# A hybrid decoder layer on one core: sums of weight quarters issued singly, token sums inside a product, a last product by token tiles

## The chip, the core and the metric

The kernel runs on one core of a Trainium2 chip. The core's engines work side by side, each through its own list of instructions in order: TensorE (PE) for matrix products, with its weight loads (PEld) overlapped; VectorE (DVE) for element work; ScalarE (ACT) for copies, casts and functions; GpSimd (POOL), here for the rsqrt powers, some fills and some DMAs; SyncE (SP), whose list issues nearly all DMAs. A DMA that must wait for something holds everything behind it in the list that issues it. The metric is the device time of one execution in microseconds (us). TensorE's clock is granted by a throttle; the trace gives it as a share of full speed.

## The reference, cut to what matters

One layer (DEPTH is 1) over 1024 tokens and 16 meta tokens, width 1024, all in float32:

```python
h = layer_norm(concat(meta, x), emb_ln_g, emb_ln_b)
p = h @ w_in[l]                       # one input projection for four mixers
y_pool, y_rw, y_lru, y_ml = ...       # pooling, RWKV-7, RG-LRU, mLSTM
mix = jnp.concatenate([y_pool, y_rw, y_lru, y_ml], axis=-1) @ w_out[l]
h = layer_norm(ALPHA * h + mix, ln1_g[l], ln1_b[l])
ff = jnp.square(jax.nn.relu(h @ mlp_w1[l])) @ mlp_w2[l]
h = layer_norm(ALPHA * h + ff, ln2_g[l], ln2_b[l])
return h[:, N_META:]
```

The MLP is 1024 to 4096 and back to 1024.

## The kernel before

**Products.** Every float32 operand is split into a high part (cast on ACT) and a low part (original minus high, on DVE); a product is three matmuls, high x high, high x low and low x high (`mm3`, the matmuls of L1149). `split` (L125, L126) does this for data, `load_w` (L117, L120, L121) loads one 512 KB tile of weights by SP and splits it. Two raw tiles are held, so SP is at most two weight loads ahead of the split.

**The mixers.** The eight token tiles of 128 are taken in four blocks of two. A list written by hand (`PLAN`, then `STEPS`) sets the order in which the program's steps are written: `e` embedding and its LayerNorm, `S` parts of the input projection, `P`, `I`, `C` the RWKV mixer (the inverse of a triangular system, with small round trips through memory: `dr`, `XTm`, `SA`, `XT`), `L` the RG-LRU, `O` the pooling, `M` the mLSTM, `W` six parts of the output projection with the first LayerNorm (its rsqrt power runs on POOL, L133) and the store of `h1d`, `T` and `G` the first-layer product of the first half of the tokens, and `Z`. A scheduler then makes each engine's final list from the written order and the waits.

**The Z steps.** The MLP saves products in the manner of Strassen: the tokens are two halves, the weight matrices two by two quarters, and seven products of sums replace eight. Four of them need sums of quarters of the second weight w2, kept in memory as `rd1` to `rd4`, each in four pieces of 1 MB (in listings, `rd_0_207` to `rd_3_210` are rd1's pieces, 211 to 214 rd2's, 215 to 218 rd3's, 219 to 222 rd4's; `in_w` is then w2). `Z0` to `Z3` make one piece of each (`w2_sums`): SP copies a quarter to rd1, POOL issues a DMA that adds another quarter to it (an accumulating DMA, L1181); the same for rd3; then SP copies rd1 to rd2 (L1180) and POOL accumulates, then rd2 to rd4 and POOL accumulates. Each copy of one sum to the next waits for the accumulation before.

**Behind the mixers.** `mlp_sums` makes five operands of token sums (`t0` to `t4`, in the code `tops`) in transposed layout: it loads the second token half's tiles of `h1d`, transposes them on PE (L1207), copies them on ACT (L1209), forms differences with the first half's transposed tiles `h1t` on DVE (six per tile, L1213 to L1218) and splits five results per tile. Then comes `down_product("11")`, the first second-layer product, with operands loaded (L1298, L1304) and split for two of 16 steps at a time into a ring of 8 high and 8 low tiles; then 16 `mlp_set` (the first-layer products of the sums) and six more `down_product`: 21, s2, n1, s3, s4 and 22. In a `down_product` each group of two steps runs six matmuls on each of four banks of PSUM, bank after bank; a bank belongs to a token tile. While 22 runs, the first four token tiles are normed (`acc[0..3]`, L1344); after it, for each of the other four, the bank is added (L1349) and the second LayerNorm follows (statistics L145, L146; L160 and L161 apply it) and the store (L162).

Of the kernel before, what the change touches and what calls it, by code (L numbers as in the profile page):

```python
# [9 lines left out]
F32 = mybir.dt.float32  # L10
F32R = mybir.dt.float32r
# [25 lines left out]

PLAN = ("e0 Srw0.0 Srw0.1 k Srw0.2 Srw0.3 Srw0.4 Srw0.5 Srw0.6 Slp0.0 P0 I0 C0.0 Slp0.1 C0.1 Slp0.2 C0.2 "
# [52 lines left out]
class Trunk:  # L91
# [36 lines left out]
    def rsqrt(self, out, var, eps, pool, w):  # L128

        nc = self.nc  # L130
        rows = out.shape[0]
        nc.vector.tensor_scalar(out, var, eps, None, op0=ALU.add)  # L132
        nc.gpsimd.tensor_tensor(out, out, self.mhalf[0:rows, 0:w], op=ALU.pow)  # L133

    def layer_norm(self, t, rows, g, b, junk=None, pool=False, out=None, cut=1):

        nc = self.nc
        rs = self.smp.tile([P, 1], F32, name="ln_rs")
# [1 line left out]
        x = t[0:rows]  # L140
        mean, var = mv[0:rows, 0:1], mv[0:rows, 1:2]
        if junk is None:
            st = self.smp.tile([P, 2, 6], F32, name="ln_st")
            for i in range(2):
                nc.vector.bn_stats(st[0:rows, i], x[:, i * 512:(i + 1) * 512])  # L145
            nc.vector.bn_aggr(mv[0:rows], st[0:rows].rearrange("p a b -> p (a b)"))  # L146
            self.rsqrt(rs[0:rows], var, LN_EPS, self.smp, 1)
        else:
            sm = self.smp.tile([P, 2], F32, name="ln_sm")
            nc.scalar.activation(junk[0:rows], x, AF.Identity, accum_out=sm[0:rows, 0:1])  # L150
            nc.scalar.activation(sm[0:rows, 1:2], sm[0:rows, 0:1], AF.Copy, scale=-1.0 / D ** 1.5)
            nc.scalar.activation(mean, sm[0:rows, 0:1], AF.Copy, scale=1.0 / D)
            nc.scalar.activation(junk[0:rows], x, AF.Square, scale=D ** -0.5, bias=sm[0:rows, 1:2], accum_out=var)
            nc.gpsimd.tensor_tensor(rs[0:rows], var, self.eps[0:rows], op=ALU.add)
            nc.gpsimd.tensor_tensor(rs[0:rows], rs[0:rows], self.mhalf[0:rows, 0:1], op=ALU.pow)
# [126 lines left out]
    def program(self, top):  # L282
# [36 lines left out]
        self.rws, self.mls, self.lrs = ([{} for b in range(nb)] for i in range(3))  # L319
        M, M2 = ExitStack(), ExitStack()  # L320
        for st in STEPS:
            t, i = (st.split(".") + ["0"])[0:2]
            k, b, i = t[0], int(t[-1]) if t[-1].isdigit() else None, int(i)
            if k == "k":
# [5 lines left out]
            elif k == "T":  # L330
                self.mlp_in()
            elif k == "G":
                self.mlp_first(int(t[1:]))
            elif k == "Z":
                self.w2_sums(b)
            elif k == "C":
                self.rwkv_chunk(b, i)
            elif k == "M":
                if i == 0:
                    self.mlstm_pre(b)  # L340
                else:
                    self.mlstm_chunk(b, i - 1)
            elif k == "S":
                self.sweep(b, t[1:3], i)
            elif k == "W":
                self.w_out(b, i)
            else:
                {"e": self.emb, "P": self.rwkv_pre, "I": self.rwkv_inverse, "L": self.lru, "O": self.pool}[k](b)
        X.close()
        M2.close()  # L350
        L.close()
        psc = psum(top, "psC")
        self.bank = [psc.tile([P, 512], F32, name="bank%d" % i) for i in range(8)]
        U, U2, DD = ExitStack(), ExitStack(), ExitStack()
        self.wcp = pool(DD, "wc")
        self.ring = 8
        self.p1s = [pool(DD, "p1s%d" % i).tile([P, 512], F32, name="p1s") for i in range(4)]
        self.tp = pool(U, "tops")
        tmp = ExitStack()
        self.tmp = pool(tmp, "tprep", "right")  # L360
        self.mlp_sums()
        self.down_product("11", 0, self.bank[4:8], True)
        for i in range(4):
            nc.scalar.copy(self.p1s[i], self.bank[4 + i])
        tmp.close()
# [802 lines left out]
        nc.vector.tensor_tensor(m, m, m, op=ALU.mult)  # L1168
        nc.sync.dma_start(self.md["11"][k], m)

    def w2_sums(self, j):

        nc, w2 = self.nc, self.a["w2"]
        q = lambda f, d: w2[16 * f + 4 * j:16 * f + 4 * j + 4, :, 512 * d:512 * d + 512].rearrange("n p c -> (n p) c")
        r = {i: self.rd[i][j] for i in self.rd}
        jobs = ((1, q(0, 0), q(0, 1)), (3, q(0, 1), q(1, 1)), (2, r[1], q(1, 1)), (4, r[2], q(1, 0)))
        last = self.last_dma
        for i, first, more in jobs:
            with self.tc.issue_after(last):
                nc.sync.dma_start(r[i], first)  # L1180
            nc.gpsimd.dma_start(r[i], more, accum_op=ALU.add)  # L1181

    def half_split(self, pool, name, out_h, out_l, src, neg=False):
        nc = self.nc
        if neg:
            nc.scalar.activation(out_h, src, AF.Copy, scale=-1.0)
            nc.vector.scalar_tensor_tensor(out_l, src, -1.0, out_h.bitcast(F32), op0=ALU.mult, op1=ALU.subtract)
        else:
            self.split(out_h, out_l, src)

    def mlp_sums(self):

        nc, tmp = self.nc, self.tmp
        self.tops = [[self.tp.tile([P, 4, 512], F32R, name="t%d%s" % (q, x)) for x in "hl"] for q in range(5)]
        bh, bl = self.h1t
        v = lambda x: x.rearrange("p (a b) -> p a b", b=P)
        tt = nc.vector.tensor_tensor
        for i in range(4):
            cs = slice(i * P, (i + 1) * P)
            x = tmp.tile([P, D], F32, name="h1x", bufs=2)  # L1200
            nc.sync.dma_start(x, self.h1d[4 + i])
            b = []
            for half in range(2):
                pt = self.bank[2 * (i % 2) + half]
                for j in range(4):
                    kt = half * 4 + j
                    nc.tensor.transpose(pt[:, j * P:(j + 1) * P], x[:, kt * P:(kt + 1) * P], self.ident)  # L1207
                y = tmp.tile([P, 512], F32, name="b%d2" % half)
                nc.scalar.copy(y, pt)  # L1209
                b.append(y)  # L1210
            t1, t2, t3, t4 = (tmp.tile([P, 512], F32, name="tt%d" % q) for q in range(4))
            h = lambda z, k: z[:, 4 * k:4 * k + 4, cs].bitcast(F32)
            tt(v(t1), v(b[0]), h(bh, 0), op=ALU.subtract)  # L1213
            tt(v(t1), v(t1), h(bl, 0), op=ALU.subtract)
            tt(t2, b[1], t1, op=ALU.subtract)  # L1215
            tt(t3, b[0], b[1], op=ALU.subtract)
            tt(v(t4), h(bh, 1), v(t2), op=ALU.subtract)
            tt(v(t4), v(t4), h(bl, 1), op=ALU.add)  # L1218
            for q, z in ((1, t2), (0, t1), (2, t3), (4, b[1]), (3, t4)):
                self.half_split(tmp, "t", self.tops[q][0][:, :, cs], self.tops[q][1][:, :, cs], v(z), neg=(q == 4))  # L1220

        for i in range(2):
            nc.tensor.matmul(self.bank[i], lhsT=self.identr, rhs=self.tops[0][0][:, 0], start=True, stop=True)

    def pair(self, src):
        hi = self.wcp.tile([P, 512], F32R, name="wh", bufs=self.ring)
# [61 lines left out]
        for q, y in zip(("n1", "s2", "s3", "s4"), o):  # L1288
            nc.sync.dma_start(self.md[q][k], y)

    def down_product(self, q, w, banks, start, group=2):

        nc, w2 = self.nc, self.a["w2"]
        for g in range(0, NS, group):
            ops = []
            for k in range(g, g + group):
# [14 lines left out]
    def mlp_out(self, ap):  # L1311
# [26 lines left out]
        for i in R4:  # L1338
            tt(v7[i], X[i], self.p1s[i], op=ALU.add)
            tt(v7[i], v7[i], y5[i], op=ALU.add)  # L1340
            stt(acc[4 + i][:, hi], acc[4 + i][:, hi], ALPHA, v7[i], op0=ALU.mult, op1=ALU.subtract)
        self.down_product("22", 4, X, False)
        for i in R4:
            tt(v[i], v[i], Y[i], op=ALU.add)  # L1344
            stt(acc[i][:, hi], acc[i][:, hi], ALPHA, v[i], op0=ALU.mult, op1=ALU.subtract)
# [1 line left out]
        for i in R4:  # L1347
            t = 4 + i
            tt(acc[t][:, lo], acc[t][:, lo], X[i], op=ALU.add)  # L1349
# [54 lines left out]
```

## Time and profile before

| | us |
|---|---|
| median of three runs | 1393.0 (1391.18 to 1403.27) |
| the profiled execution | 1390.15 |
| its span in the trace | 1388.1 |
| PE busy | 1249.0 (90%) |
| DVE busy | 868.5 (63%) |
| ACT busy | 616.7 (44%) |
| POOL busy | 91.7 (7%) |

The profiled execution is 2.85 us below the median of the runs. Its mean granted clock is 0.931 of full speed. Times in the trace count from the span's start. The mixers end near 814, the products run from 848 to 1372, and the final LayerNorms end at 1388. A row of the trace names the source line, the engine, the operation and the tiles as output<-input; in brackets is the engine's idle time before it, and what ended it.

### The profile page before, as it was taken

Reading aid. Unit: us, or ns where it says so; the run is one execution under the profiler, and the core shown is the slowest. Engines: PE = TensorE matmul, PEld = TensorE weight load, DVE = VectorE, ACT = ScalarE, POOL = GpSimd, SP = SyncE. Lnnn points to the kernel's source line nnn. Section 1 sums busy time; section 2 is a strip of 40 time slices with the busy share of each in tenths; the row PEclk is TensorE's granted clock in tenths of the full one; section 3 lists DMA queues with packets and bytes.
Section 4 is the critical chain, followed back from the end, with each engine's and each line's share of the span. In section 5 each row is a group of like instructions: output and inputs, shape, how many; then the busy total and the mean of one; then the engine's idle time right before and its main releaser. Section 6 shows DMA issues by size and latency. Waiting matters only on the chain. (4 is left out here: it accounts for less than half of the span.)

```text
span 1388.1 us, 21003 instructions
## 1 busy us (share of the span) xinstructions
PE 1249.0 (90%) x7619; PEld 1065.3 (77%) x7619; DVE 868.5 (63%) x2122; ACT 616.7 (44%) x1128; POOL 91.7 (7%) x117
## 2 busy tenths in 40 slices
PE   4999988999986977999699666999999999999995
PEld 3989877898986965775587654888888888888884
DVE  8847645776634654554576477676767556545697
ACT  5436464452355442434233244465666643443431
POOL 3110010000100010002001000000000000000011
PEclk9999997899997977997889787999999999999998
DMA  7422267252496469527943455667666587656662
GB/s 249 164 81 74 73 170 195 96 144 62 137 253 188 137 201 224 183 69 202 240 137 108 131 191 174 187 222 243 226 229 235 197 304 250 195 187 200 192 220 114
DMA packets 122599, 245.84 MB, mean 177 GB/s; under 512 B 28768, under 2 KB 35568, under 8 KB 122368
## 3 DMA queue, kind: packets, MB, share of 16 engines
q1 hardware_dynamic: 114048, 227.73, 49.5%
q0 software_dynamic: 8448, 16.78, 7.3%
q8 instruction: 60, 0.98, 0.3%
q14 instruction: 43, 0.35, 0.1%
HBM read 193.07 MB, written 84.94 MB: 200 GB/s over the span
## 5 line engine op out<-in xcount | busy, mean ns | idle before, releaser
L126 DVE TENSOR_TENSOR wl<-raw,wh 128x512 fp32r<-128x512 f32 x240 | 151.5, 685 | 121.3 <-ACT wh L125 121.2
L125 ACT CAST wh<-raw 128x512 fp32r<-128x512 f32 x240 | 133.5, 618 | 196.0 <-PE bank L1149 189.7
L452 PE MATMUL b<-hTh,wlo 128*128 128x256 f32 (+1 forms) x672 | 195.5, 291 | 1.9 <-DVE wlo L121 1.9
L451 PE MATMUL b<-hTl,whi 128*128 128x256 f32 (+1 forms) x672 | 196.5, 293 | 0.6 <-DVE hTl L126 0.4
L450 PE MATMUL b<-hTh,whi 128*128 128x256 f32 (+1 forms) x672 | 195.9, 292 | 0.2 <-ACT hTh L125 0.2
L1149 PE MATMUL bank<-wl,wh 128*128 128x512 f32 x448 | 175.4, 392 | 4.2 <-DVE wl L126 4.2
L1149 PE MATMUL bank<-wh 128*128 128x512 f32 x448 | 175.3, 393 | 1.1 <-ACT wh L125 1.1
L1149 PE MATMUL bank<-wh,wl 128*128 128x512 f32 x448 | 175.2, 391 | 0.0
L121 DVE TENSOR_TENSOR wlo<-wraw,whi 128x1024 fp32r<-128x1024 f32 x90 | 109.7, 1220 | 102.6 <-ACT whi L120 101.1
L120 ACT CAST whi<-wraw 128x1024 fp32r<-128x1024 f32 x90 | 94.3, 1047 | 146.4 <-PE b L451 42.6
L452 PEld LDWEIGHTS b<-hTh,wlo 128*128 128x128 f32 x672 | 129.8, 193 | 3.8 <-DVE wlo L121 2.7
L451 PEld LDWEIGHTS b<-hTl,whi 128*128 128x128 f32 x672 | 129.8, 193 | 3.8 <-issue 1.5
L450 PEld LDWEIGHTS b<-hTh,whi 128*128 128x128 f32 x672 | 130.0, 193 | 1.5 <-ACT hTh L125 0.7
L1149 PEld LDWEIGHTS bank<-wl,wh 128*128 128x128 f32 x448 | 84.7, 189 | 22.7 <-DVE wl L126 5.2
L1149 PEld LDWEIGHTS bank<-wh 128*128 128x128 f32 x448 | 84.8, 190 | 19.2 <-ACT wh L125 1.5
L1149 PEld LDWEIGHTS bank<-wh,wl 128*128 128x128 f32 x448 | 84.7, 189 | 17.4
L1127 PE MATMUL b<-whi,mixh 128*128 128x256 f32 x256 | 76.3, 300 | 12.3 <-ACT mixh L125 9.6
L1128 PE MATMUL b<-wlo,mixh 128*128 128x256 f32 x256 | 77.6, 303 | 2.2 <-DVE wlo L121 2.2
L133 POOL TENSOR_TENSOR ln_rs<-ln_rs,mhalf 128x1 f32<-128x1 f32 (+1 forms) x22 | 31.0, 1410 | 709.4 <-DVE ln_rs L132 709.4
L1129 PE MATMUL b<-whi,mixl 128*128 128x256 f32 x256 | 76.6, 301 | 0.0
L126 DVE TENSOR_TENSOR wl<-s,wh 128x512 fp32r<-128x512 f32 x64 | 43.7, 688 | 33.0 <-ACT wh L125 33.0
L1127 PEld LDWEIGHTS b<-whi,mixh 128*128 128x128 f32 x256 | 51.6, 202 | 13.3 <-ACT mixh L125 9.9
(424 smaller groups left out, 2562.9 us busy)
## 6 DMA issues: line engine op xcount, KB each, us to landing
wraw<-in_w_in SPq DMA_DIRECT2D x42, 512.0 KB, 3.5
rd<-in_w POOLq DMA_DIRECT2D x16, 1024.0 KB, 10.9
wraw<-in_w_out SPq DMA_DIRECT2D x32, 512.0 KB, 3.6
raw<-in_w SPq DMA_DIRECT2D x32, 512.0 KB, 4.3
raw<-rd SPq DMA_DIRECT2D x64, 256.0 KB, 3.8
md<-m SPq DMA_DIRECT2D x48, 256.0 KB, 2.0
raw<-md SPq DMA_DIRECT2D x48, 256.0 KB, 4.0
raw<-in_w SPq DMA_DIRECT2D x48, 256.0 KB, 4.1
```

The costliest lines, as they stand in the source:

```text
L120: nc.scalar.copy(hi, raw)
L121: (nc.gpsimd if pool else nc.vector).tensor_tensor(lo, raw, hi.bitcast(F32), op=ALU.subtract)
L125: self.nc.scalar.copy(hi, src)
L126: self.nc.vector.tensor_tensor(lo, src, hi.bitcast(F32), op=ALU.subtract)
L133: nc.gpsimd.tensor_tensor(out, out, self.mhalf[0:rows, 0:w], op=ALU.pow)
L450: nc.tensor.matmul(pt, lhsT=wh[:, ks], rhs=hh[:, kt, 0:nb], start=(kt == 0), stop=False)
L451: nc.tensor.matmul(pt, lhsT=wh[:, ks], rhs=hl[:, kt, 0:nb], start=False, stop=False)
L452: nc.tensor.matmul(pt, lhsT=wl[:, ks], rhs=hh[:, kt, 0:nb], start=False, stop=(kt == 7))
L1127: nc.tensor.matmul(pt, lhsT=xh, rhs=wh, start=(kt == 0), stop=False)
L1128: nc.tensor.matmul(pt, lhsT=xh, rhs=wl, start=False, stop=False)
L1129: nc.tensor.matmul(pt, lhsT=xl, rhs=wh, start=False, stop=(kt == 7))
L1149: mm = lambda *p, **k: self.nc.tensor.matmul(*p, skip_group_check=True, **k)
```

## The change

Three things change. Behind the change the line numbers of the profile shift by some 5 to 14.

1. The four Z steps go. Their 32 transfers become single steps (`SUMS`; C a copy by SP, A an accumulation by POOL), put into `STEPS` one at every fourth place from place 16: all copies of rd1 and rd3, all their accumulations, the copies of rd2, its accumulations, then rd4. A copy is placed in SP's list right behind the weight load written last, an accumulation in POOL's behind the rsqrt power written last.
2. `mlp_sums(i)` works on one token tile: it loads that tile of both halves, forms four differences in token layout before the transposes (on POOL for tiles 0 and 1, on DVE for 2 and 3), transposes five results (20 transposes per tile, 80 in all, where there were 32), and splits them straight from PSUM. Between the four calls stand two groups each of product 11.
3. The ring is 20 from `mlp_out` on, and the last product's last group holds eight of the 16 steps, so that each bank gets its last 24 matmuls in one run. The statistics of the half of each last tile that is ready earlier are taken ahead.

```diff
+SUMS = [(k, i, j) for q in ((1, 3), (2,), (4,)) for k in "CA" for i in q for j in range(4)]
+for n, z in enumerate(SUMS):
+    STEPS.insert(16 + 4 * n, z)
...
-        nc.gpsimd.tensor_tensor(out, out, self.mhalf[0:rows, 0:w], op=ALU.pow)
+        self.last_pool = nc.gpsimd.tensor_tensor(out, out, self.mhalf[0:rows, 0:w], op=ALU.pow).ins
...
+            if isinstance(st, tuple):
+                self.w2_sum(*st)
+                continue
...
-        self.mlp_sums()
-        self.down_product("11", 0, self.bank[4:8], True)
+        for i in range(4):
+            self.mlp_sums(i)
+            self.down_product("11", 0, self.bank[4:8], True, range(4 * i, 4 * i + 4, 2))
...
+        self.wcp, self.ring = pool(DD, "wd"), 20
...
-        for i, first, more in jobs:
-            with self.tc.issue_after(last):
-                nc.sync.dma_start(r[i], first)
-            nc.gpsimd.dma_start(r[i], more, accum_op=ALU.add)
+    def w2_sum(self, k, i, j):
+        if k == "C":
+            with self.tc.issue_after(self.last_dma):
+                nc.sync.dma_start(r[i][j], {1: q(0, 0), 3: q(0, 1), 2: r[1][j], 4: r[2][j]}[i])
+        else:
+            with self.tc.issue_after(self.last_pool):
+                nc.gpsimd.dma_start(r[i][j], {1: q(0, 1), 3: q(1, 1), 2: q(1, 1), 4: q(1, 0)}[i], accum_op=ALU.add)
...
+        nc.sync.dma_start(x2, self.h1d[4 + i])
+        nc.sync.dma_start(x1, self.h1d[i])
+        tt = (nc.gpsimd if i < 2 else nc.vector).tensor_tensor
+        tt(t1, x2[:, lo], x1[:, lo], op=ALU.subtract)
+        tt(t2, x2[:, hi], t1, op=ALU.subtract)
+        tt(t3, x2[:, lo], x2[:, hi], op=ALU.subtract)
+        tt(t4, x1[:, hi], t2, op=ALU.subtract)
+        for q, z in ((4, x2[:, hi]), (0, t1), (1, t2), (2, t3), (3, t4)):
+            pt = self.bank[self.nt % 4]
+            for j in range(4):
+                nc.tensor.transpose(pt[:, j * P:(j + 1) * P], z[:, j * P:(j + 1) * P], self.ident)
...
+            nc.vector.bn_stats(sts[i][:, 1], acc[4 + i][:, hi])
-        self.down_product("22", 4, X, False)
+        self.down_product("22", 4, X, False, [0, 2, 4, 6, 8])
```

What this does to the engines' lists shows at three places. On SP, around the step Z1 of before (`wraw` are weight loads, `x<-h0d` a load of the residual):

```order
L1180 DMA rd_1_208<-in_w 512x512
L1180 DMA rd_1_216<-in_w 512x512
L117 DMA wraw<-in_w_in 128x1024
L1180 DMA rd_1_212<-rd_1_208 16x16384
L117 DMA wraw<-in_w_out 128x1024
L1180 DMA rd_1_220<-rd_1_212 16x16384
L117 DMA wraw<-in_w_out 128x1024 x2
```

and the corresponding place in the changed list, about the output projection of block 1:

```order
L122 DMA wraw<-in_w_in 128x1024
L1191 DMA rd_0_211<-rd_0_207 16x16384
L1124 DMA x<-h0d_66 128x1024
L122 DMA wraw<-in_w_in 128x1024
L1191 DMA rd_1_212<-rd_1_208 16x16384
L122 DMA wraw<-in_w_out 128x1024 x3
L1078 DMA yd_316<-sc_4695 128x2x256
L122 DMA wraw<-in_w_out 128x1024
L122 DMA wraw<-in_w_in 128x1024
L1191 DMA rd_2_213<-rd_2_209 16x16384
```

Between a copy and the next one there are now one or more other loads, and rd2's copies stand there alone: rd1's accumulations were issued far ahead. In the same way the copies of rd1 and rd3 stand earlier among input weight loads, the first copy of rd3 and some of rd1 just ahead of the small transfers of the first RWKV inverse.

On POOL, the end of the list before, with the rsqrt powers of the last LayerNorms (`ln_rs`; in one row with those of the final norms) and of the last head norms:

```order
L133 TENSOR_TENSOR ln_rs<-ln_rs,mhalf 128x1
L133 TENSOR_TENSOR ml_rs<-ml_rs,mhalf 128x4
L133 TENSOR_TENSOR ln_rs<-ln_rs,mhalf 128x1
L133 TENSOR_TENSOR rw_rs<-rw_rs,mhalf 128x4 x2
L133 TENSOR_TENSOR ln_rs<-ln_rs,mhalf 128x1 x10
```

and now (`tt` are the token differences, `h1x` the loaded token tiles):

```order
L1194 DMA rd_2_221<-in_w 512x512
L138 TENSOR_TENSOR rw_rs<-rw_rs,mhalf 128x4
L1210 TENSOR_TENSOR tt_8590<-h1x_8585 128x512
L1208 TENSOR_TENSOR tt_8588<-h1x_8585,h1x_8584 128x512
L1209 TENSOR_TENSOR tt_8589<-h1x_8585,tt_8588 128x512
L1211 TENSOR_TENSOR tt_8591<-h1x_8584,tt_8589 128x512
L1210 TENSOR_TENSOR tt_8724<-h1x_8719 128x512
L1208 TENSOR_TENSOR tt_8722<-h1x_8719,h1x_8718 128x512
L1209 TENSOR_TENSOR tt_8723<-h1x_8719,tt_8722 128x512
L1211 TENSOR_TENSOR tt_8725<-h1x_8718,tt_8723 128x512
L138 TENSOR_TENSOR ln_rs<-ln_rs,mhalf 128x1 x10
```

The two accumulations of rd4 and the eight differences now stand ahead of the last ten powers, two of which belong to the first LayerNorm of the last block.

On DVE, the norms of the last token tiles at the end of the list before (`L1349` adds the bank):

```order
L1349 TENSOR_TENSOR acc_11534<-acc_11534,bank_8549 128x512
L145 BN_STATS ln_st<-acc_11534 128x6
L1349 TENSOR_TENSOR acc_11535<-acc_11535,bank_8550 128x512
L146 BN_AGGR ln_mv<-ln_st 128x2
L145 BN_STATS ln_st<-acc_11535 128x6
L132 TENSOR_SCALAR ln_rs<-ln_mv 128x1
L160 SCALAR_TENSOR_TENSOR acc_11534<-acc_11534,ln_mv,bc_ln2g 128x1024
L145 BN_STATS ln_st<-acc_11535 128x6
L161 SCALAR_TENSOR_TENSOR acc_11534<-acc_11534,ln_rs,bc_ln2b 128x1024
L146 BN_AGGR ln_mv<-ln_st 128x2
L1349 TENSOR_TENSOR acc_11536<-acc_11536,bank_8551 128x512
```

and now, where `L1356` adds the bank and `st_` are the statistics:

```order
L1356 TENSOR_TENSOR acc_11561<-acc_11561,bank_8550 128x512
L153 BN_STATS st_11577<-acc_11561 128x6
L154 BN_AGGR ln_mv<-st_11577 128x2
L137 TENSOR_SCALAR ln_rs<-ln_mv 128x1
L168 SCALAR_TENSOR_TENSOR acc_11561<-acc_11561,ln_mv,bc_ln2g 128x1024
L169 SCALAR_TENSOR_TENSOR acc_11561<-acc_11561,ln_rs,bc_ln2b 128x1024
L1356 TENSOR_TENSOR acc_11562<-acc_11562,bank_8551 128x512
L153 BN_STATS st_11578<-acc_11562 128x6
L154 BN_AGGR ln_mv<-st_11578 128x2
L137 TENSOR_SCALAR ln_rs<-ln_mv 128x1
L168 SCALAR_TENSOR_TENSOR acc_11562<-acc_11562,ln_mv,bc_ln2g 128x1024
L169 SCALAR_TENSOR_TENSOR acc_11562<-acc_11562,ln_rs,bc_ln2b 128x1024
```

Before, the tiles' steps are interleaved; now a tile's steps stand together, and one statistic is taken after each addition instead of two.

More of the change, by code (lines that the diff above doesn't have):

```diff
@@ L132, in rsqrt, with layer_norm @@
         nc.vector.tensor_scalar(out, var, eps, None, op0=ALU.add)
-        nc.gpsimd.tensor_tensor(out, out, self.mhalf[0:rows, 0:w], op=ALU.pow)
-    def layer_norm(self, t, rows, g, b, junk=None, pool=False, out=None, cut=1):
+        self.last_pool = nc.gpsimd.tensor_tensor(out, out, self.mhalf[0:rows, 0:w], op=ALU.pow).ins
+    def layer_norm(self, t, rows, g, b, junk=None, pool=False, out=None, cut=1, st=None):
         nc = self.nc
@@ L142, in layer_norm @@
         if junk is None:
-            st = self.smp.tile([P, 2, 6], F32, name="ln_st")
-            for i in range(2):
+            n = 2 if st is None else 1
+            if st is None:
+                st = self.smp.tile([P, 2, 6], F32, name="ln_st")
+            for i in range(n):
                 nc.vector.bn_stats(st[0:rows, i], x[:, i * 512:(i + 1) * 512])
@@ L333, in program @@
                 self.mlp_first(int(t[1:]))
-            elif k == "Z":
-                self.w2_sums(b)
             elif k == "C":
@@ L350, in program @@
         M2.close()
+        M.close()
         L.close()
@@ L354, in program @@
         U, U2, DD = ExitStack(), ExitStack(), ExitStack()
-        self.wcp = pool(DD, "wc")
-        self.ring = 8
-        self.p1s = [pool(DD, "p1s%d" % i).tile([P, 512], F32, name="p1s") for i in range(4)]
+        p1p = pool(DD, "p1")
+        self.p1s = [p1p.tile([P, 512], F32, name="p1s%d" % i) for i in range(4)]
+        wc = ExitStack()
+        self.wcp, self.ring = pool(wc, "wc"), 8
         self.tp = pool(U, "tops")
@@ L360, in program @@
         self.tmp = pool(tmp, "tprep", "right")
-        self.mlp_sums()
-        self.down_product("11", 0, self.bank[4:8], True)
+        self.nt = 0
+        for i in range(4):
+            self.mlp_sums(i)
+            self.down_product("11", 0, self.bank[4:8], True, range(4 * i, 4 * i + 4, 2))
         for i in range(4):
@@ L365, in program @@
         tmp.close()
-        M.close()
         self.stp = pool(U2, "stage", "right")
@@ L372, in program @@
         U2.close()
+        wc.close()
+        self.wcp, self.ring = pool(DD, "wd"), 20
         self.mlp_out(pool(DD, "acc", "right"))
@@ L1169, in mlp_first @@
         nc.sync.dma_start(self.md["11"][k], m)
-    def w2_sums(self, j):
-        nc, w2 = self.nc, self.a["w2"]
+    def w2_sum(self, k, i, j):
+        nc, w2, r = self.nc, self.a["w2"], self.rd
         q = lambda f, d: w2[16 * f + 4 * j:16 * f + 4 * j + 4, :, 512 * d:512 * d + 512].rearrange("n p c -> (n p) c")
-        r = {i: self.rd[i][j] for i in self.rd}
-        jobs = ((1, q(0, 0), q(0, 1)), (3, q(0, 1), q(1, 1)), (2, r[1], q(1, 1)), (4, r[2], q(1, 0)))
-        last = self.last_dma
-        for i, first, more in jobs:
-            with self.tc.issue_after(last):
-                nc.sync.dma_start(r[i], first)
-            nc.gpsimd.dma_start(r[i], more, accum_op=ALU.add)
@@ L1183, in half_split @@
[L1183 to L1187, printed above, removed]
-        else:
-            self.split(out_h, out_l, src)
-    def mlp_sums(self):
+        if k == "C":
+            with self.tc.issue_after(self.last_dma):
+                nc.sync.dma_start(r[i][j], {1: q(0, 0), 3: q(0, 1), 2: r[1][j], 4: r[2][j]}[i])
+        else:
+            with self.tc.issue_after(self.last_pool):
+                nc.gpsimd.dma_start(r[i][j], {1: q(0, 1), 3: q(1, 1), 2: q(1, 1), 4: q(1, 0)}[i], accum_op=ALU.add)
@@ L1193, in mlp_sums @@
+    def mlp_sums(self, i):
         nc, tmp = self.nc, self.tmp
[L1194 to L1220, printed above, removed]
@@ L1222, in mlp_sums @@
-        for i in range(2):
-            nc.tensor.matmul(self.bank[i], lhsT=self.identr, rhs=self.tops[0][0][:, 0], start=True, stop=True)
+        if i == 0:
+            self.tops = [[self.tp.tile([P, 4, 512], F32R, name="t%d%s" % (q, x)) for x in "hl"] for q in range(5)]
+        cs = slice(i * P, (i + 1) * P)
+        x1, x2 = (tmp.tile([P, D], F32, name="h1x%d" % k, bufs=2) for k in range(2))
+        nc.sync.dma_start(x2, self.h1d[4 + i])
+        nc.sync.dma_start(x1, self.h1d[i])
+        t1, t2, t3, t4 = (tmp.tile([P, 512], F32, name="tt%d" % q, bufs=2) for q in range(4))
@@ new lines, in mlp_sums @@
+        tt = (nc.gpsimd if i < 2 else nc.vector).tensor_tensor
+        lo, hi = slice(0, 512), slice(512, 1024)
+        tt(t1, x2[:, lo], x1[:, lo], op=ALU.subtract)
[4 more added lines that the diff above has]
+            pt = self.bank[self.nt % 4]
+            self.nt += 1
+            for j in range(4):
+                nc.tensor.transpose(pt[:, j * P:(j + 1) * P], z[:, j * P:(j + 1) * P], self.ident)
+            v = pt.rearrange("p (a b) -> p a b", b=P)
+            h, l = (x[:, :, cs] for x in self.tops[q])
+            if q == 4:
+                nc.scalar.activation(h, v, AF.Copy, scale=-1.0)
+                nc.vector.scalar_tensor_tensor(l, v, -1.0, h.bitcast(F32), op0=ALU.mult, op1=ALU.subtract)
+            else:
+                self.split(h, l, v)
@@ L1225, in pair @@
+        if i == 3:
+            for k in range(2):
+                nc.tensor.matmul(self.bank[k], lhsT=self.identr, rhs=self.tops[0][0][:, 0], start=True, stop=True)
     def pair(self, src):
@@ L1289, in mlp_set, with down_product @@
             nc.sync.dma_start(self.md[q][k], y)
-    def down_product(self, q, w, banks, start, group=2):
+    def down_product(self, q, w, banks, start, groups=range(0, NS, 2)):
         nc, w2 = self.nc, self.a["w2"]
-        for g in range(0, NS, group):
+        for g, end in zip(groups, [*groups[1:], groups.stop if isinstance(groups, range) else NS]):
             ops = []
-            for k in range(g, g + group):
+            for k in range(g, end):
                 raw = self.wcp.tile([P, 1024], F32, name="raw", bufs=4)
@@ L1318, in mlp_out @@
         v, v7, y5 = new("v"), new("v7"), new("y5")
+        sts = [ap.tile([P, 2, 6], F32, name="st%d" % i) for i in range(4)]
         for t in range(NT):
@@ L1349, in mlp_out @@
             tt(acc[t][:, lo], acc[t][:, lo], X[i], op=ALU.add)
-            self.layer_norm(acc[t], P, g2, b2, out=a["out"][t * P:(t + 1) * P], cut=2 if i == 3 else 1)
+            self.layer_norm(acc[t], P, g2, b2, out=a["out"][t * P:(t + 1) * P], cut=2 if i == 3 else 1, st=sts[i])
 def _layout(inp):
```

6 rows, old and new, of the table PLAN are left out of this document.

## The prediction

> **What bounds the kernel now.** I read the busy slices of the page first, to see where TensorE (PE) stands still.
>
> ```profile
> PE   4999988999986977999699666999999999999995
> PEclk9999997899997977997889787999999999999998
> DMA  7422267252496469527943455667666587656662
> ```
>
> PE is full nearly everywhere. The holes are slices 6 and 7, 12 and 13, 15 and 16 and 20 (in the mixers), 23 to 25 (their end and the change to the second-layer products) and the last. Where PE idles its granted clock drops too, so a pause costs more than its idle time. The table of stretches puts numbers on this (us, then PE, PEld, DVE, ACT, POOL busy, clock, DMA share, GB/s); first three undisturbed stretches of the mixers, then the four in which a Z step issues its transfers, the transition, the products, the tail:
>
> ```profile
> 260.00:380.00 120.00, 116.87 (x1026) 105.99 (x1025) 89.34 (x316) 49.39 (x93) 10.63 (x18) 1.00 0.35 106
> 440.00:500.00 60.00, 59.70 (x503) 59.43 (x502) 41.06 (x88) 27.08 (x41) 2.98 (x2) 1.00 0.43 145
> 540.00:620.00 80.00, 78.41 (x529) 60.15 (x528) 46.04 (x161) 30.17 (x59) 3.46 (x5) 1.00 0.51 149
> 180.00:260.00 80.00, 71.89 (x447) 62.97 (x447) 44.33 (x144) 39.71 (x79) 9.73 (x14) 0.79 0.69 185
> 380.00:440.00 60.00, 44.63 (x320) 42.45 (x319) 19.25 (x27) 31.68 (x46) 4.11 (x4) 0.83 0.87 231
> 500.00:540.00 40.00, 22.60 (x110) 17.08 (x109) 18.32 (x57) 14.61 (x34) 5.56 (x5) 0.62 0.92 233
> 620.00:700.00 80.00, 64.11 (x292) 45.81 (x290) 41.15 (x162) 24.56 (x54) 9.39 (x14) 0.78 0.76 200
> 812.00:848.00 36.00, 11.29 (x57) 8.44 (x55) 35.01 (x58) 20.75 (x37) 2.99 (x2) 0.64 0.35 124
> 848.00:1372.00 524.00, 523.69 (x2300) 433.17 (x2300) 333.24 (x532) 258.25 (x463) 7.72 (x5) 1.00 0.66 218
> 1372.00:1388.00 16.00, 0.00 (x0) 0.00 (x0) 13.08 (x22) 0.00 (x0) 4.00 (x4) 0.59 0.33 131
> ```
>
> I call length minus busy time times clock the lost time: the work PE could have done there at full clock. The three undisturbed stretches lose 5.0 of 260 us. The Z stretches lose 80 - 71.89 x 0.79 = 23.2, then 23.0, 26.0 and 30.0, together 102, also of 260 us. The products lose nothing, so only fewer matmuls would shorten them, and their number stays. The transition loses 36 - 11.29 x 0.64 = 28.8, the tail all its 16.
>
> Why the Z stretches stall, the waits of the queues tell (total us, times, longest), with the issues of the sync engine's queue (SP) around Z1:
>
> ```profile
> SPq L1180 <- DMA rd<-in_w: 113.3, 8, 16.8
> POOL rd L1181 <- DMA rd<-rd: 104.8, 8, 14.7
> ...
> 386.66 0.34 SPq L117 DMA_DIRECT2D wraw<-in_w_in  x1
> 401.96 0.47 SPq L1180 DMA_DIRECT2D rd<-rd  x1
> 402.54 0.52 SPq L117 DMA_DIRECT2D wraw<-in_w_out  x1
> 419.36 0.47 SPq L1180 DMA_DIRECT2D rd<-rd  x1
> ```
>
> After 386.66 SP issues nothing for 15 us: its next entry copies rd1 to rd2 and waits for the accumulation just issued to end. The mixers' next weight loads stand behind it, one slips through at 402.54, and the same happens until 419.36. It is a wait in an in-order queue, eight times, 113.3 us in all.
>
> **Part 1, the sums one by one.** The bytes and the 32 transfers stay; what goes is the wait, since in the new order no copy stands right behind the accumulation that it reads. At most the excess of the Z stretches is won, 102 - 5 = 97. If the lower clock were all due to something else, the idle time alone is won: (8.1 + 15.4 + 17.4 + 15.9) - 5.0 = 52. Which end is nearer, a count tells: 380 to 440 holds 320 matmuls, its neighbour 440 to 500 holds 503 in 59.7 busy us, so (503 - 320) x 59.7 / 503 = 21.7 us of work is missing, nearly all of that stretch's 23.0. I take 85.
>
> What the spread transfers cost afterwards is in no row of its own. The nearest:
>
> ```profile
> q0 software_dynamic: 8448, 16.78, 7.3%
> ...
> wraw<-in_w_in SPq DMA_DIRECT2D x42, 512.0 KB, 3.5
> rd<-in_w POOLq DMA_DIRECT2D x16, 1024.0 KB, 10.9
> rd<-in_w SPq DMA_DIRECT2D x8, 1024.0 KB, 10.0
> ...
> 380.00:400.00 20.00, 19.95 (x162) 19.54 (x161) 5.69 (x5) 12.97 (x21) 2.09 (x2) 1.00 0.99 287
> ...
> 468.56 12.21 SPq L117 DMA_DIRECT2D wraw<-in_w_in  x4
> ```
>
> A load behind a copy lands up to 10.0 - 3.5 = 6.5 us later. Four loads in 12.21 us are one per about 4.0, and two raw tiles are held, so some 8 us of cover: a lone copy is hidden, barely. Lower end of the cost 0 (at 380 to 400 the DMA engines are 0.99 busy and PE is 19.95 of 20), upper end 6.5 for each of 16 copies, 104. I take 1 us for each of 11 copies among loads (nearest the row with PE full); for the five copies of rd1 and rd3 that now stand just ahead of the small round trips of the first RWKV inverse (dr, XTm, SA, XT), which have no cover, half of 6.5 each, 15; and 5 for the accumulations issued in bunches of three and four, which carry 10.9 us each beside the loads. Sum about 30, so the mixers win 85 - 30 = **55**; with 55 of cost 30, with 5 of it 80. The copies of rd2 and rd4 also lie on SP ahead of stores (yd, md) and second-layer inputs; these have the transfers' time as slack, and I add nothing. On POOL the accumulations wait for copies issued long before; if one had not landed, the rsqrt powers behind it, and VectorE (DVE) after them, would wait.
>
> The Trainium skill ("DMA: Bandwidth & Descriptors", section "Issuing engines are not separate DMA queues") says that transfers started by SP or GpSimd run on the same 16 DMA engines and interleave. By that alone the Z stretches would stay DMA-bound wherever the transfers are issued, and little would be won; the 0.99 row with PE full speaks against it, the shares of 0.87 and 0.92 in stalled stretches for it. It is the first rival below.
>
> **Part 2, the token sums.** Before the first matmul of the product that has a low weight half stands the DVE:
>
> ```profile
> 814.00 0.60 PE L1207 MATMUL bank<-cst,h1x 128*128 128x128 f32 x4
> 842.77 1.22 PE L1223 MATMUL bank<-t0h,identr 128*128 128x512 f32 x2 [8.73 <-ACT t0h L125]
> 848.14 0.80 PE L1149 MATMUL bank<-wl,wh 128*128 128x512 f32 x1 [4.15 <-DVE wl L126]
> ...
> 826.93 0.68 DVE L1213 TENSOR_TENSOR tt<-b,h1Th 128x512 f32<-128x512 f32 x1
> 827.53 0.68 DVE L1216 TENSOR_TENSOR tt<-b,b 128x512 f32<-128x512 f32 x1
> ...
> 804.73 0.33 SPq L117 DMA_DIRECT2D wraw<-in_w_out  x1
> ...
> 10.82 2.54 POOL L167 TENSOR_TENSOR x<-x,bc_b 16x1024 f32<-16x1024 f32 x1 [3.17 <-ACT x L166]
> ```
>
> DVE has 24 subtractions and 20 splits ahead of it at a pitch of 0.60 us (826.93 to 827.53). In the new order 10 splits, one negated low half (t4l) and 3 subtractions stand there, 30 fewer, 18 us. That is partly given back: eight subtractions move to POOL ahead of the rsqrt powers of the last two LayerNorms. POOL's two-input row takes 2.54 for 1024 columns, so I estimate 1.27 for 512 and 10 us for eight; only what is not done by 814 holds the last LayerNorms, about 4. The last weight load of W3.5 (804.73) now stands behind two h1x loads and a store: 2. So the stream starts about 12 earlier, at 836. Into it go 24 transposes of 0.15 (0.60 for four), 3.6, and about 1 of waiting on their operands. Gain **7.5**, from 12 down to -2: the h1x loads of tiles 6 and 7 remain behind the last LayerNorms anyway, and POOL at 2.5 each would hold those another 10 us.
>
> The Trainium skill ("GPSIMD Engine Reference", section "1. Specifications") says that GpSimd's SBUF interfaces are shared with VectorE, in contention with DVE instructions of two SBUF inputs. No row here shows a POOL subtraction beside the DVE; by that rule part 2 wins about 0 and the sum comes out at 1328.
>
> **Part 3, the last product by token tiles.** The tail before:
>
> ```profile
> 1371.22 0.39 PE L1149 MATMUL bank<-wl,wh 128*128 128x512 f32 x1
> 1371.44 0.39 PE L1149 MATMUL bank<-wh,wl 128*128 128x512 f32 x1
> ...
> 1367.79 0.69 DVE L1349 TENSOR_TENSOR acc<-acc,bank 128x512 f32<-128x512 f32 x1 [4.56 <-PE bank L1149]
> 1368.51 0.69 DVE L145 BATCH_NORM_STATS2 ln_st<-acc 128x6 f32<-128x512 f32 x1
> 1379.10 1.27 DVE L160 SCALAR_TENSOR_TENSOR acc<-acc,ln_mv,bc_ln2g 128x1024 f32<-128x1024 f32 x1
> 1382.08 0.20 DVE L146 BATCH_NORM_AGGREGATE ln_mv<-ln_st 128x2 f32<-128x12 f32 x1
> ```
>
> All four banks end within the last group, so four LayerNorms queue on DVE after 1367.79. From the last matmul's end (1371.83) to the span's end (1388.1) are 16.3 us. In the new order a bank ends every 24 matmuls, at a step of 0.22 (1371.22 to 1371.44) 5.3 us. One tile's norm is an addition and a statistic of 0.69, 0.20 for their collection and two passes of 1.27, 4.1 us, so it ends inside that, and only the last tile's is left: 0.69, 0.69, and 6.0 from 1382.08 to the end, 7.4. Gain 8.9 if DVE is ready; it also has the four norms of acc[0..3] and 16 splits in that time, so I take **8**, from 5 to 9. The ring of 20 hides the splits: they are made while the group before runs; without that cover 16 x 0.60 = 9.6 would be lost.
>
> **Sum.** 55 + 7.5 + 8 = 70.5. The profiled execution took 1390.15 (span 1388.1); it is 2.85 below the median of the runs, 1393.0. 1390.15 - 70.5 = 1319.65, about 1320.
>
> **Rivals.**
> 1. *The bandwidth is the limit, not the order.* For it: 0.87 and 0.92 in the stalled stretches; against it: 0.99 with PE full. The mixers win 20 to 30 only: 1390 - (20..30) - 15.5 = 1345 to 1355, to 1372 if parts 2 and 3 give nothing.
> 2. *All of the excess comes back*, 97, with the upper ends 12 and 9: 1272; between that and 1295.
> 3. *Slower: every single transfer delays the load behind it.* SP then loses a little 32 times instead of much eight times. It decides from (85 + 15.5) / 32 = 3.1 us each. The upper bound of 6.5 is above that, the cover of 8 us against it. At 4.5 each it is 144 - 100.5, 44 us slower: 1434.
> 4. *The copies do not leave the stalls*, because accumulations are late and each copy waits as before: parts 2 and 3 alone, 1375. The order speaks against it: other loads stand between.
>
> **How the numbers follow.** Forecast, with 80 to 30 from the mixers and 15.5 from the rest (1295 to 1345), 0.68; rivals 1 and 4 (1345 to 1376) 0.20; rival 2 (below 1295) 0.08; rival 3 0.04. The predicted time is 1320. The range 1288 to 1352 leaves out some of rival 2, half of rival 1, and rival 3. A measurement of this kernel tells about 1% from no change, so faster means below 1379: 0.92; within 1% 0.05, from late rival 1 and mild rival 3; slower 0.03.
>
> **What would show it.** SP's wait at the copy line falls from 113 us to under 30; stretches at 180 to 260, 380 to 440, 500 to 540 and 620 to 700 vanish as holes; PE's mean clock rises; the start of the products comes about 62 us earlier; POOL's subtractions last 1.3 each; after the last matmul 7 to 8 us remain. Wrong if weight loads in the mixers land in over 8 us, if the first inverse is later by more than 15, or if POOL holds the last LayerNorms for 10 us or more.

## The result and the profile after

| | before | changed |
|---|---|---|
| median of the runs, us | 1392.69 | 1351.68 (1348.88 to 1355.6, 4 runs) |
| the profiled execution, us | 1390.15 | 1348.88 |
| its span, us | 1388.1 | 1347.0 |
| mean granted clock | 0.931 | 0.951 |

The ratio of the runs is 0.9692, with a 95% interval of 0.9638 to 0.9745. The kernel is faster by 41 us where 73 were forecast from the median (70.5 in the sum); the time lies just inside the upper edge of the range, 1352, and two of the four runs lie above it.

The page of the changed kernel, busy slices as before (PE, its clock, DMA):

```profile
PE   4999999899979988999989679999999999999997
PEclk9999998897999996998889789999999999999999
DMA  7545323841497485724555567676767588766652
```

The holes are shallower, and not gone: the clock still dips in slices 7, 8, 10, 16, 19 to 21, 23 and 24. For numbers, here are the stretches of the mixers again. Their bounds are set so that each holds the same PE work as its counterpart before (summed from the matmuls' shapes), which the numbers of matmuls confirm within 4%. First column bounds and length, then PE, PEld, DVE, ACT, POOL busy, clock, DMA share, GB/s:

```profile
180.00:250.00 70.00, 65.53 (x453) 57.81 (x452) 44.03 (x144) 38.27 (x77) 8.67 (x13) 0.88 0.46 128
250.00:381.00 131.00, 124.34 (x1025) 112.41 (x1025) 90.61 (x316) 51.10 (x95) 15.89 (x23) 0.93 0.49 129
381.00:434.00 53.00, 43.83 (x318) 41.64 (x318) 18.55 (x27) 32.63 (x47) 1.05 (x1) 0.94 0.90 254
434.00:495.00 61.00, 59.89 (x502) 59.40 (x501) 38.68 (x82) 25.17 (x37) 5.04 (x4) 1.00 0.59 182
495.00:530.00 35.00, 24.21 (x109) 17.47 (x107) 20.82 (x64) 15.40 (x37) 3.42 (x3) 0.61 0.76 213
530.00:609.00 79.00, 78.51 (x530) 60.44 (x530) 45.69 (x158) 29.84 (x59) 2.39 (x4) 1.00 0.45 146
609.00:666.00 57.00, 54.32 (x281) 39.90 (x280) 37.67 (x146) 24.28 (x52) 6.54 (x11) 0.91 0.52 151
666.00:792.00 126.00, 107.80 (x782) 94.43 (x780) 68.59 (x200) 35.47 (x58) 20.27 (x17) 0.85 0.55 156
```

The last of these in the kernel before, from 700 on:

```profile
700.00:814.00 114.00, 100.21 (x770) 88.96 (x770) 65.10 (x182) 34.77 (x57) 7.51 (x8) 0.90 0.42 133
```

Lost time (length minus busy time times clock) in the four Z stretches is now 12.3, 11.8, 20.2 and 7.6, together 52 where it was 102. So 50 us were won there. But the stretches between them, which lost 5, now lose 15.4, 1.1 and 0.5, and the last one, up to the end of the mixers, loses 34.4 where the same work lost 23.8 before. About 23 us of the 50 are given back inside the mixers, and they win some 28, not 55. The bounds alone say 22 (634 us from 180 on before, 612 now); the measure of lost time multiplies two means and is not exact. SP's list of waits has no row for the copies any more, where it had 113.3 us. POOL waits once, 29.2 us for the first copy of rd2, but its next power comes only 70 us later.

Not all of these losses are pauses. In the kernel before, PE stands still from 224.5 to 228.4 in Z0's stretch, and then runs at half clock while it is busy without a gap; in the changed kernel the same happens later, and no pause stands before it:

```profile
231.00:253.00 22.00, 22.00 (x101) 18.71 (x100) 12.50 (x36) 7.04 (x19) 1.64 (x2) 0.50 0.55 165
```

```profile
308.00:320.00 12.00, 12.00 (x55) 9.81 (x56) 3.16 (x15) 1.89 (x6) 0.00 (x0) 0.50 0.00 0
```

The first spell is 11 of the 23.2 us that Z0's stretch lost, the second 6 of the 15.4 of its stretch now.

The transition and the tail of the changed kernel (start, length, engine, line; in brackets the idle time before and what ended it):

```profile
783.20 1.89 POOL L1210 TENSOR_TENSOR tt<-h1x 128x512 f32<-128x512 f32 x1 [36.32 <-PE b L1143]
...
796.51 1.28 DVE L177 SCALAR_TENSOR_TENSOR x<-x,ln_rs,bc_b 128x1024 f32<-128x1024 f32 x1 [2.41 <-POOL ln_rs L138]
...
811.75 0.48 PE L1163 MATMUL bank<-wl,wh 128*128 128x512 f32 x1
...
1338.79 0.39 PE L1163 MATMUL bank<-wh,wl 128*128 128x512 f32 x1
...
1339.22 0.69 DVE L1356 TENSOR_TENSOR acc<-acc,bank 128x512 f32<-128x512 f32 x1 [0.67 <-PE bank L1163]
1342.31 1.41 DVE L169 SCALAR_TENSOR_TENSOR acc<-acc,ln_rs,bc_ln2b 128x512 f32<-128x512 f32 x2
```

The stream of products starts at 811.75 where it was 848.14. POOL's eight differences run from 783.20 to 795.96 and hold the LayerNorm's power, for which DVE waits 2.41. From the last matmul's end (1339.18) to the span's end (1347.0) are 7.8 us, 16.3 before, with the last addition 0.04 behind it.

### The profile page after: what moved, and what is told of

The parts are those of the page before. It is cut to its first block, busy times and chain, and to the rows that moved or that the text cites. A ratio compares the mean times of both kernels' runs of the same rounds, so it can differ in the third digit from the quotient of the medians.

```text
span 1347.0 us, 21089 instructions
## 1 busy us (share of the span) xinstructions
PE 1252.3 (93%) x7667; PEld 1069.4 (79%) x7667; DVE 862.6 (64%) x2106; ACT 613.6 (46%) x1120; POOL 104.6 (8%) x125
```

## Experiments

Two theories stood after the traces. A: the stalls were the Z steps as counted, and the spread transfers still cost most of it. B: a good part of the stalls were other waits of the mixers, and the spread transfers cost little. Ratios compare with runs of the kernel before on the same chip. The changed kernel was measured only beside its own runs of the kernel before (1392.69), so the differences from its 1351.68 below are rough; by the ratios they are 1 to 5 us larger.

### Without the sums, on either kernel

The four products that used sums read plain quarters, with the same loads:

```diff
-for n, z in enumerate(SUMS):
-    STEPS.insert(16 + 4 * n, z)
...
-                    src = self.rd[w][k // 4][(k % 4) * P:(k % 4 + 1) * P]
+                f, d = {0: (0, 0), 5: (1, 0), 6: (1, 1), 1: (0, 1), 2: (1, 1), 3: (0, 1), 4: (1, 0)}[w]
+                src = w2[16 * f + k][:, 512 * d:512 * d + 512]
```

> The changed kernel with the 32 transfers of the sums left out; the four products that read sums read plain quarters of w2 instead, with the same number of loads of the same size, so the output is not the reference's. Theory A (the stalls of the four stretches were the Z steps, worth 85, and the spread transfers still cost most of that: 85 less the 23 that the mixers won): 60 us below the changed kernel, about 1290 us. Theory B (a good part of the stalls were other waits of the mixers, their small round trips and chains, which only moved; the spread transfers cost little now): 10 to 15 us below the changed kernel, about 1338 us.

Measured: 1321.05 us, ratio 0.9463 (0.9426 to 0.95).

The kernel before, with the Z steps taken from its list and the same reads:

> The kernel before with the Z steps left out in the same way (plain quarters of w2 are read, the output is not the reference's). Theory A: 85 us below the kernel before, about 1308 us. Theory B: about 40 us below it, 1353 us.

Measured: 1337.55 us against 1395.25, ratio 0.9584 (0.9549 to 0.9619).

So the Z steps cost 57.7 us in the kernel before, and the spread transfers cost 1351.68 - 1321.05 = 30.6 in the changed one (32 by the ratios, whose intervals leave some 9 us either way). Neither theory had both numbers: A had too much of each, B too little (40 and 10 to 15). The stretches of the kernel before without sums, cut at equal work like those above, and one more line, 301 to 325:

```profile
181.00:245.00 64.00, 60.22 (x444) 53.03 (x443) 43.63 (x143) 39.43 (x79) 5.78 (x10) 0.95 0.32 100
245.00:375.00 130.00, 126.98 (x1024) 114.96 (x1023) 89.57 (x316) 49.30 (x93) 10.73 (x18) 0.91 0.32 97
375.00:417.00 42.00, 40.98 (x325) 39.52 (x324) 19.31 (x28) 32.76 (x48) 0.00 (x0) 1.00 0.42 136
476.00:504.00 28.00, 20.04 (x110) 14.45 (x109) 17.99 (x56) 14.46 (x34) 2.38 (x2) 0.76 0.41 127
583.00:642.00 59.00, 56.33 (x284) 41.16 (x283) 38.12 (x147) 24.32 (x52) 5.51 (x10) 0.88 0.40 128
...
301.00:325.00 24.00, 24.00 (x107) 20.77 (x107) 8.59 (x36) 4.81 (x13) 1.01 (x1) 0.50 0.07 22
```

With no transfer of a sum at all, the four stretches still lose 6.8, 1.0, 12.8 and 9.4, together 30, not the 5.0 of undisturbed stretches. The one at 476 has only 110 matmuls, about half of them in the small chains of the third block's RWKV, and stalls by itself. And the stretch from 245 loses 14.4 where it lost 3.1: its last line shows PE busy all of 24 us at a clock of 0.50. So 102 - 30 = 72 went with the sums, and some 11 of these come back as a spell of half clock. The kernel before has none at this place, but has the one of 22 us in Z0's stretch, which is not there without sums. A spell of nearly the same size stands in either kernel, so its 11 us were counted as Z0's and not won.

Where the 30 lie shows in the changed kernel without sums, at the stretches that belong to 180, 381, 495 and 666 of the changed kernel:

```profile
182.00:248.00 66.00, 62.18 (x449) 54.97 (x448) 44.28 (x144) 40.05 (x79) 5.78 (x10) 0.92 0.31 97
380.00:421.00 41.00, 39.97 (x316) 38.43 (x315) 18.48 (x27) 32.31 (x47) 0.00 (x0) 1.00 0.41 133
480.00:509.00 29.00, 22.04 (x113) 16.04 (x112) 18.17 (x57) 14.53 (x34) 2.38 (x2) 0.71 0.39 122
649.00:764.00 115.00, 97.50 (x774) 84.72 (x775) 67.45 (x195) 35.53 (x58) 16.76 (x14) 0.94 0.45 141
```

They lose 8.8, 1.0, 13.4 and 23.4. With the transfers they lost 12.3, 11.8, 20.2 and 34.4, so the transfers cost 3.5, 10.8, 6.8 and 11.0 there; the other stretches give some 3 back.

### The parts of the change

The first part alone, on the kernel before (the edits of `SUMS`, `w2_sum` and `last_pool`, no others):

> The kernel before with the first part of the change alone. Both theories, from the traces of the two kernels (equal PE work is reached 23 us earlier at the end of the mixers): about 1370 us. The prediction's own term: 55 us below, 1338 us.

Measured: 1362.73 us against 1395.25, 32.5 less, ratio 0.9768 (0.9724 to 0.9813). The second and third part alone, the changed kernel with the Z steps as before:

> The changed kernel with the four Z steps as before, so the second and third part of the change alone. The prediction's terms 7.5 and 8: 1377 us. If the parts help each other (the first part moves what stands at the transition): 1380 or more.

Measured: 1379.51 us, 15.7 less, ratio 0.9883 (0.9839 to 0.9926). The two terms 7.5 and 8 hold in their sum (the interval leaves 10 to 22; the two kernels without sums differ by 16.5), the 55 does not. The two sets of parts add up to 48, some 5 more than the 43 that the change as a whole has by its ratio.

### Is it the queue or the transfers?

```diff
-                nc.sync.dma_start(r[i], first)
+                (nc.gpsimd if i in (2, 4) else nc.sync).dma_start(r[i], first)
```

> The kernel before, with the eight copies from one sum to the next issued by POOL in place of SP; transfers, bytes and their order among themselves stay, SP no longer waits for an accumulation. Theory Q (the Z steps cost what they do because SP's queue stands still): most of what the spread kept is won here too, 25 to 35 us below the kernel before, about 1364 us. Theory D (the transfers themselves crowd the DMA engines): within 8 us of the kernel before, about 1390 us. If POOL's waits ahead of its powers cost more than SP's did: slower than before.

Measured: 1384.22 us against 1396.33, ratio 0.9897 (0.983 to 0.9963): neither. The stretches are of two kinds. Z1's and Z0's, cut at equal work, and POOL's list around Z0:

```profile
394.00:436.00 42.00, 40.80 (x321) 39.12 (x320) 18.93 (x27) 32.45 (x47) 3.64 (x4) 1.00 1.00 271
182.00:262.00 80.00, 66.23 (x448) 58.53 (x447) 44.12 (x145) 39.93 (x79) 10.86 (x16) 0.85 0.72 185
...
204.11 0.53 POOL L1180 DMA_DIRECT2D rd<-rd  x1 [5.04 <-DMA rd<-in_w]
204.66 1.05 POOL L133 TENSOR_TENSOR rw_rn<-rw_rn,mhalf 128x4 f32<-128x4 f32 x1
211.60 1.05 POOL L1181 DMA_DIRECT2D rd<-in_w  x1 [4.98 <-DMA rd<-rd]
212.72 1.03 POOL L133 TENSOR_TENSOR rw_rn<-rw_rn,mhalf 128x4 f32<-128x4 f32 x1
```

At Z1 the DMA engines now run at a share of 1.00, and PE is busy 40.80 of 42 us: lost 1.2, where it was 23.0 with SP waiting. Two of Z1's eight transfers now come later, in the stretch from 436 to 502, which loses 6.3 where it lost 0.3; that leaves some 16 of the 23 that SP's wait is shown to have cost. At Z0 two powers of the RWKV normalisation stand on POOL behind the waits (204.66, 212.72), PE waits 9.3 and 2.3 us for them (3.8 in the kernel before), and the stretch still loses 23.7; Z2's goes from 26.0 to 22.7, Z3's from 30.0 to 35.4. The wait was moved to another queue that is waited for. The execution that this trace shows took 1390.19, no less than before: a half-clock spell from 316 to 344 took back most of what Z1 won.

### What the spread transfers still cost

```diff
+            if st[0:2] == ("A", 3):
+                continue
             if isinstance(st, tuple):
```

> The changed kernel without the four accumulations of rd3, which stand back to back on POOL; rd3 stays a plain quarter, so the output is not the reference's. Bunch theory (four accumulations at once delay the weight loads; equal work is reached 11 us later there than without any sums): 10 to 12 us below the changed kernel, about 1341 us. Even theory (each of 32 transfers costs its share of 30 us): 4 us below, about 1348 us.

Measured: 1337.01 us, 14.7 below the changed kernel, ratio 0.9576 (0.9515 to 0.9637). The bunch in the changed kernel (POOL's issues, PE's first long wait after, the landing times of the weight loads from 365 to 425), then the stretch without it:

```profile
369.56 4.20 POOL L1194 DMA_DIRECT2D rd<-in_w  x4
392.47 0.49 PE L464 MATMUL b<-hTh,whi 128*128 128x256 f32 x1 [4.74 <-ACT ml_q L543]
DMA to landing us min/median/max: 8.0/11.4/14.7
...
381.00:422.00 41.00, 39.98 (x316) 38.52 (x315) 18.58 (x27) 32.30 (x47) 1.08 (x1) 1.00 0.71 222
```

With four accumulations issued within 4.20 us, weight loads land after 8.0 to 14.7; without them, those from 360 to 420 land after 3.5 to 5.5, and the stretch loses 1.0 and not 11.8.

The same with one accumulation:

```diff
+            if st == ("A", 4, 3):
+                continue
             if isinstance(st, tuple):
```

> The changed kernel without the last accumulation of rd4 alone, which POOL issues at 686 us just ahead of a small round trip of the last RWKV inverse; the last quarter of rd4's rows stays as rd2's, so the output is not the reference's. Round-trip theory (one transfer of 1 MB ahead of the small ones makes that chain wait): 6 to 9 us below the changed kernel, about 1344 us. Even theory: 1 us, no difference that can be measured.

Measured: 1346.63 us, 5.1 below, but the intervals overlap (0.9565 to 0.9695), so the time alone decides nothing. The trace does, for the round trip of the last inverse (`dr` out, `SA` in). In the changed kernel, with the accumulation, and then without it:

```profile
686.19 1.08 POOL L1194 DMA_DIRECT2D rd<-in_w  x1
690.01 2.77 SPq L717 DMA_DIRECT2D dr<-ys  x4
699.67 1.82 SPq L720 DMA_DIRECT2D SA<-dr  x4
```

```profile
697.45 2.52 SPq L719 DMA_DIRECT2D dr<-ys  x4
703.40 1.82 SPq L722 DMA_DIRECT2D SA<-dr  x4
```

From the first issue of `dr` to that of `SA` are 9.7 us with one transfer of 1 MB ahead and 5.95 without. In the first case the clock falls too: the last stretch loses 34.4 with it and 22.9 without. In this profile a half-clock spell at 307 to 335, longer than that of the changed kernel, took back 6 of it, and the execution was no faster (1351.22 against 1348.88).

A transfer of 1 MB ahead of a round trip is not always dear. The first inverse has five copies ahead of it, one of them issued by SP at 125.50, and its round trip takes 4.2 us in the changed kernel, 4.1 in the kernel before:

```profile
128.26 2.56 SPq L717 DMA_DIRECT2D dr<-ys  x4
132.42 2.90 SPq L720 DMA_DIRECT2D SA<-dr  x4
```

PE is busy 39.4 of 40 us there, from 100 to 140, in both kernels.

### Elsewhere than in the mixers

rd1 and rd3 are spread wider, rd2 and rd4 are issued one transfer per set, where PE has a long dense stretch:

```diff
+SUMS = [(k, i, j) for k in "CA" for i in (1, 3) for j in range(4)]
+for n, z in enumerate(SUMS):
+    STEPS.insert(16 + 7 * n, z)
...
-        nc.sync.dma_start(xa, self.a["w1"][k])
+        self.last_dma = nc.sync.dma_start(xa, self.a["w1"][k]).ins
+        self.w2_sum("CA"[k % 2], 2 + k // 8 * 2, k // 2 % 4)
```

> The changed kernel with the sums rd1 and rd3 spread wider over the mixers (one transfer at every seventh place) and rd2 and rd4 issued one transfer per first-layer set of the second token half, behind that set's weight load, where PE is full and the DMA share is about 0.66. If the sets have room: the mixers pay about 10 of 30 us and the sets nothing, about 1332 us. If they have none: the sets' loads come late and it ends at 1350 or above.

Measured: 1334.58 us (1325.71 to 1335.54), ratio 0.9536 (0.9474 to 0.9598): the fastest here of all kernels that compute the whole layer, its interval clear of the changed kernel's. Then 24 and all 32 transfers in the sets (the list in `mlp_set` taken as three per two sets, and two per set):

> Only rd1's eight transfers stay in the mixers, one at every fourteenth place; the other 24 are issued in the sixteen first-layer sets, three in every two sets. In the run with 16 in the sets their DMA share went from 0.68 to 0.90 with PE at 279.0 of 279 us, so 24 give about 1.01. If only full DMA engines make PE wait: the sets lose a few us, the mixers win the rest of what the sums cost there, and it stays within 6 us of the run with 16, 1330 to 1340 us. If queue order counts in the sets too: over 1345.

Measured: 1346.3 us (one of the four runs at 1334.08, the others at 1345.57 to 1347.18), ratio 0.9608 (0.9544 to 0.9671): 12 slower than with 16, twice what was expected; the intervals overlap. The two traces do not settle the 12: that with 24 has a half-clock spell from 304 to 328, that with 16 has none there.

> All 32 transfers in the sets, two in each, none in the mixers. The DMA share would be 0.68 + 32 x (0.22 / 16) = 1.12, more than there is, so the bandwidth must now bound: 0.12 x 280 = 34 us lost in the sets against the run without any sums (1321), about 1355 us. If it comes out near 1325, the DMA engines were not the limit at any load tried.

Measured: 1353.35 us, ratio 0.968 (0.9621 to 0.9739), two below the expectation. The sets with 16, 24 and 32 transfers, in that order:

```profile
787.00:1066.00 279.00, 279.00 (x1239) 230.42 (x1240) 191.09 (x302) 166.36 (x297) 8.18 (x8) 1.00 0.90 289
```

```profile
800.00:1076.00 276.00, 269.80 (x1184) 221.29 (x1183) 181.22 (x288) 157.73 (x283) 12.23 (x12) 0.99 0.98 310
```

```profile
784.00:1060.00 276.00, 257.60 (x1096) 206.53 (x1096) 169.48 (x270) 144.42 (x264) 16.44 (x16) 0.98 1.03 316
```

At a share of 0.90 PE waits for nothing; at 0.98 it loses 276 - 269.80 x 0.99 = 9, at 1.03 it is 24. With 32, DVE waits 53 us in all for the sets' weights to land, and no copy on SP waits for an accumulation. This is the bandwidth as a limit, and in the sets it begins only there. The changed kernel's mixers are at 0.45 to 0.76 in all of their stretches from 180 on but one (0.90). But these are averages. Behind the bunch the DMA engines are full too, and PE stands:

```profile
372.00:400.00 28.00, 21.46 (x162) 20.51 (x161) 6.42 (x9) 5.38 (x10) 2.42 (x4) 0.94 1.13 274
```

## Why the prediction was right and wrong

**The wait in SP's queue.** The mechanism was right: the rows at the copies are gone, and at Z1 some 16 of 23 us are shown to be the queue's, with the DMA engines at a share of 1.00. The step that failed is the term "I take 85", set toward the top of 52 to 97 by the count of missing matmuls. Measured, the Z steps cost 57.7. The count says that PE's work is missing, not who is to blame for it. It was made at Z1, the one stretch where without sums almost nothing is lost (1.0), and carried to the other three, where 6.8, 12.8 and 9.4 stay for reasons of their own; and 11 us, counted as Z0's, were a spell of half clock that without sums comes at another place. The lower end, 52, which takes the low clock for something else, was the nearer one.

**The cost of the spread transfers.** The 30 hold in sum (30.6), not in their places, so the sum is luck. Five copies ahead of the first inverse were given 15 (five halves of 6.5 are 16): it came 0.2 us later than in the kernel before, so they cost nothing there. The bunches were given 5: the four accumulations at 369.56 alone cost 11 to 15, and the one at 686.19 ahead of the last inverse 5 by the times and 11 by the trace. The last was not in the sum at all; the prediction counted copies ahead of round trips, not accumulations. With 58 in place of 85, the sum as it stands would have been 1390.15 - (58 - 30) - 15.5 = 1346.7, against 1348.88 in the profile. That the time lies in the range at all is due to its upper end, 1352, which left room for a term 27 too high. Of the signs named in advance, one of being wrong came up (loads landing in over 8 us), and the products start 36 us earlier, not 62.

**The token sums and the tail.** 7.5 + 8 = 15.5 forecast, 15.7 measured for the two together. The tail's 7.4 us is 7.8, so it gains 8.5, and the rest is the transition's. POOL held the LayerNorm 2.41 where 4 were taken. Its differences were estimated at 1.27: five took 1.26 to 1.29, three 1.89 to 2.15. The Trainium skill ("GPSIMD Engine Reference", section "1. Specifications") has GpSimd's SBUF interfaces in contention with VectorE instructions of two SBUF inputs; the three long ones agree with that in kind. Each of them (783.20, 787.78 and 792.49) starts while DVE runs an instruction that reads two SBUF tiles, and none of the five short ones does:

```profile
782.71 1.23 DVE L126 TENSOR_TENSOR wlo<-wraw,whi 128x1024 fp32r<-128x1024 f32 x1 [0.57 <-ACT whi L125]
787.47 1.31 DVE L126 TENSOR_TENSOR wlo<-wraw,whi 128x1024 fp32r<-128x1024 f32 x1 [2.42 <-ACT whi L125]
792.15 1.35 DVE L172 SCALAR_TENSOR_TENSOR x<-x,ln_mv,bc_g 128x1024 f32<-128x1024 f32 x1
```

But it took 2.4 us, not the term's whole gain, and this is one trace: no run here separates it from other causes.

**The rivals.** The time is that of the first rival (1345 to 1355), and its cause is not. It had the DMA engines as the limit; the sets of products show that limit between 0.90 and 0.98 of their share, and the mixers are under it on average. Only in bursts, as behind the four accumulations, do they meet it, and by spreading the transfers further the kernel became faster with the same bytes (1334.58). Read as a general rule, the Trainium skill's ("DMA: Bandwidth & Descriptors", section "Issuing engines are not separate DMA queues") is not contradicted: transfers of all queues did interleave, with weight loads landing after 8.0 to 14.7 us behind four accumulations. What it costs hangs on who waits at that moment. The third rival, a price on each of 32 transfers, had the form right and the price wrong: 30.6 / 32 is 1.0 each on average, far under the 3.1 from which it would have decided, and two stretches hold over two thirds of it (10.8 and 11.0).

## What to carry to other kernels

A stretch in which a wait stands is not lost to that wait alone: before counting its excess as gain, look for the chains in it that would wait anyway and for clock lost while PE is busy, or run the kernel once without the suspected work. A transfer off the critical path is free where PE runs densely on loads with slack, here up to a DMA share of 0.90, and dear in bunches and, in one of the two places looked at, just ahead of a small round trip, so spread large transfers by who waits near them and not evenly by the list. A wait is removed only when it is moved to a queue on which nothing needed stands behind it.

## What was not expected of the hardware

PE ran at a granted clock of 0.50 for spells of some 10 to 28 us while it was busy without a gap: 24.00 of 24 us at 0.50 from 301 to 325 in the old kernel without sums. The spell in Z0's stretch of the kernel before follows a pause of 3.9 us; those at 301 and 308 follow none. Kernels whose lists hardly differ there differ in it: without sums both have it, and the one with half the transfers in the sets does not (23.84 of 24 at 1.00):

```profile
301.00:325.00 24.00, 23.84 (x185) 20.38 (x185) 14.70 (x59) 7.49 (x18) 1.01 (x1) 1.00 0.15 48
```

Such a spell costs up to 14 us (28 us at 0.51 in the kernel with POOL's copies), and runs of one kernel here differ by nearly that much (1325.71 at a mean clock of 0.965, 1335.54 at 0.953; only the first has a trace). What sets it off was not tried and stays open. It took back about 11 of the gain of the kernel before without sums.
